# Instance norm over 512 volumes: loads and stores on two queues, six buffers, and a two-pass variance in one chain per tile

## The chip, the cores and the metric

The kernel runs on one core of one Trainium2 chip. The metric is device time in microseconds (us) of one execution; lower is better.

## The reference

The input `x` has shape (8, 64, 32, 64, 64) in float32: 512 instances (8 batches of 64 channels) of 131,072 elements each, 268.44 MB in all. Every instance is normalised by its own mean and variance.

```python
def reference(x, eps):                       # eps = 1e-5
    mean = np.mean(x, axis=(2, 3, 4), keepdims=True)
    var = np.var(x, axis=(2, 3, 4), keepdims=True)
    return ((x - mean) / np.sqrt(var + eps)).astype(np.float32)
```

## The kernel before

A tile is 128 partitions by 8192 elements (`F`), 4 MB in float32. It holds 8 instances, each spread over 16 partitions (`SPLIT`), and lies in one contiguous piece in memory, as 128 rows of 32 KB. The 64 tiles are worked through in one loop; `KPG` is 1, so a group is one tile.

For each tile, `issue_load` puts a load on SyncE's queue (SP). `issue_compute` then does the following:

- VectorE (DVE) sums all 8192 elements of a partition (L92), while ScalarE (ACT) squares them, writes the squares to a scratch tile that nobody reads, and collects their sum (L100).
- TensorE multiplies the two columns of sums with `ones_t`, a block matrix that adds up the 16 partitions of an instance and hands the result to each of them (L108).
- VectorE turns the totals into mean and mean of squares (L117), squares the mean (L128), and forms the variance plus eps as the difference (L131); ScalarE takes the root (L141); VectorE makes the reciprocal `scale` (L147) and `bias`, minus mean times scale (L149).
- The tile is scaled in place by three engines side by side: VectorE the first 1024 columns (L169), ScalarE the next 1024 (L161), GpSimd (POOL) the remaining 6144 (L169).

`issue_store` (L180) puts the store on the same SP queue. The main loop issues the store of tile g - 2 (`LAG`) after the load of tile g, so this one queue carries loads and stores in turn, and a store that waits for its tile's scaling holds back the load behind it. The pool `data` has four buffers, so the load of tile g also waits until the store of tile g - 4 has landed. The tile framework orders the instructions within each engine and adds the semaphores.

Of the kernel before, what the change touches and what calls it, by code (L numbers as in the profile page):

```python
# [1 line left out]

# [4 lines left out]


@with_exitstack
def kernel(  # L10
    ctx: ExitStack,
    tc: tile.TileContext,
    x: bass.AP,
    eps: bass.AP,
    out: bass.AP,
):
    nc = tc.nc
    fp32 = mybir.dt.float32

    P = 128  # L20
    B, C, D, H, W = x.shape
    n_inst = B * C
    n_elem = D * H * W

    eps_f = float(eps)

    SPLIT = 16
    IPT = P // SPLIT
    F = n_elem // SPLIT

    G = 8
    KPG = G // IPT
    n_groups = n_inst // G

    LAG = 2

    x_packed = x.rearrange("b c d h w -> (b c) (d h w)").rearrange(
        "(k i) (s f) -> k (i s) f", i=IPT, s=SPLIT
    )
    out_packed = out.rearrange("b c d h w -> (b c) (d h w)").rearrange(  # L40
        "(k i) (s f) -> k (i s) f", i=IPT, s=SPLIT
    )

    singles = ctx.enter_context(tc.tile_pool(name="singles", bufs=1))
    data_pool = ctx.enter_context(tc.tile_pool(name="data", bufs=4))
    scratch_pool = ctx.enter_context(tc.tile_pool(name="scratch", bufs=2))
    stat_pool = ctx.enter_context(tc.tile_pool(name="stats", bufs=4))
    psum_pool = ctx.enter_context(tc.tile_pool(name="psum", bufs=4, space=bass.MemoryType.PSUM))

    ones_t = singles.tile([P, P], fp32)  # L50
    nc.vector.memset(ones_t, 1.0 / SPLIT)  # L51
    blk_pattern = [[-SPLIT, P // SPLIT], [0, SPLIT]]
    nc.gpsimd.affine_select(  # L53
        out=ones_t,
        in_=ones_t,
        pattern=blk_pattern,
        compare_op=mybir.AluOpType.is_ge,
        fill=0.0,
        base=0,
        channel_multiplier=1,  # L60
    )
    nc.gpsimd.affine_select(  # L62
        out=ones_t,
        in_=ones_t,
        pattern=[[SPLIT, P // SPLIT], [0, SPLIT]],
        compare_op=mybir.AluOpType.is_ge,
        fill=0.0,
        base=SPLIT - 1,
        channel_multiplier=-1,
    )  # L70

    inv_F = 1.0 / F

    c1 = F // 8
    c2 = F // 4
    norm_splits = [
        (nc.vector, 0, c1),
        (nc.scalar, c1, c2),
        (nc.gpsimd, c2, F),
    ]  # L80

    def issue_load(g):
        x_tiles = data_pool.tile([P, KPG, F], fp32, name="x_tiles")
        src = x_packed[g * KPG : (g + 1) * KPG].rearrange("k p f -> p k f")
        nc.sync.dma_start(out=x_tiles, in_=src)
        return x_tiles

    def issue_compute(g, x_tiles):
        psums = stat_pool.tile([P, KPG, 2], fp32, name="psums")

        for k in range(KPG):
            nc.vector.reduce_sum(  # L92
                out=psums[:, k, 0:1],
                in_=x_tiles[:, k, :],
                axis=mybir.AxisListType.X,
            )
            sq_scratch = scratch_pool.tile(
                [P, F], mybir.dt.bfloat16, name="sq_scratch"
            )
            nc.scalar.activation(  # L100
                out=sq_scratch,
                in_=x_tiles[:, k, :],
                func=mybir.ActivationFunctionType.Square,
                accum_out=psums[:, k, 1:2],
            )

        tot = psum_pool.tile([P, KPG, 2], fp32, name="tot")
        nc.tensor.matmul(  # L108
            out=tot,
            lhsT=ones_t,  # L110
            rhs=psums,
            start=True,
            stop=True,
        )

        me2 = stat_pool.tile([P, KPG, 2], fp32, name="me2")
        nc.vector.tensor_scalar(  # L117
            out=me2,
            in0=tot,
            scalar1=inv_F,  # L120
            scalar2=None,
            op0=mybir.AluOpType.mult,
        )
        mean = me2[:, :, 0]
        e2 = me2[:, :, 1]

        msq = stat_pool.tile([P, KPG], fp32, name="msq")
        nc.vector.tensor_mul(out=msq, in0=mean, in1=mean)  # L128

        var_eps = stat_pool.tile([P, KPG], fp32, name="var_eps")  # L130
        nc.vector.scalar_tensor_tensor(  # L131
            out=var_eps,
            in0=e2,
            scalar=eps_f,
            in1=msq,
            op0=mybir.AluOpType.add,
            op1=mybir.AluOpType.subtract,
        )

        std = stat_pool.tile([P, KPG], fp32, name="std")  # L140
        nc.scalar.activation(  # L141
            out=std,
            in_=var_eps,
            func=mybir.ActivationFunctionType.Sqrt,
        )
        scale = stat_pool.tile([P, KPG], fp32, name="scale")
        nc.vector.reciprocal(out=scale, in_=std)  # L147
        bias = stat_pool.tile([P, KPG], fp32, name="bias")
        nc.vector.scalar_tensor_tensor(  # L149
            out=bias,  # L150
            in0=mean,
            scalar=-1.0,
            in1=scale,
            op0=mybir.AluOpType.mult,
            op1=mybir.AluOpType.mult,
        )

        for k in range(KPG):
            for eng, lo, hi in norm_splits:
                if eng is nc.scalar:  # L160
                    nc.scalar.activation(  # L161
                        out=x_tiles[:, k, lo:hi],
                        in_=x_tiles[:, k, lo:hi],
                        func=mybir.ActivationFunctionType.Identity,
                        scale=scale[:, k : k + 1],
                        bias=bias[:, k : k + 1],
                    )
                else:
                    eng.tensor_scalar(  # L169
                        out=x_tiles[:, k, lo:hi],  # L170
                        in0=x_tiles[:, k, lo:hi],
                        scalar1=scale[:, k : k + 1],
                        scalar2=bias[:, k : k + 1],
                        op0=mybir.AluOpType.mult,
                        op1=mybir.AluOpType.add,
                    )

    def issue_store(g, x_tiles):
        dst = out_packed[g * KPG : (g + 1) * KPG].rearrange("k p f -> p k f")
        nc.sync.dma_start(out=dst, in_=x_tiles)  # L180

    pending = {}
    for g in range(n_groups):
        x_tiles = issue_load(g)
        issue_compute(g, x_tiles)
        pending[g] = x_tiles
        if g >= LAG:
            issue_store(g - LAG, pending.pop(g - LAG))
    for g in range(n_groups - LAG, n_groups):
        issue_store(g, pending.pop(g))  # L190


# [1 line left out]
_INS = ['x', 'eps']  # L194
_OUTS = [((8, 64, 32, 64, 64), 'float32')]
#: Inputs that are plain numbers.
_NUMBERS = {'eps': 9.999999747378752e-06}


# [26 lines left out]
```

## Time and profile before

| | |
|---|---|
| median of 6 runs | 1251.45 us (1250.46 to 1254.96) |
| the profiled execution | 1253.22 us; its span 1251.4 us |
| VectorE busy | 659.2 us (53%) |
| ScalarE busy | 550.6 us (44%) |
| GpSimd busy | 380.3 us (30%) |
| TensorE busy | 35.7 us (3%) |
| moved by DMA | 536.99 MB, mean 429 GB/s over the span |

The span runs from the first to the last instruction of the profiled execution; the device time also holds a little that lies around it. In the profile's rows, a line number such as L92 is that of the kernel's source. A group's row gives the engine, the operation, output and input with partitions by elements and type, the count, the busy time with the mean of one in ns, and the time the engine stood idle ahead of these instructions with what ended it. A row of the table by stretches gives the stretch, its length, the busy time of PE (TensorE), PEld (its weight loads), DVE, ACT and POOL, then the clock that TensorE was granted, the share of the DMA engines, and GB/s. "SPq" is SyncE's DMA queue. In the page's slices each column is a fortieth of the span, 31.3 us.

### The profile page before, as it was taken

What the parts mean: (1) busy time and instruction counts of PE and PEld (TensorE: products, weight loads), DVE (VectorE), ACT (ScalarE), POOL (GpSimd) and SP (SyncE); (2) the same over time, 40 slices, a digit from 0 to 9 for tenths busy, and PEclk for the clock granted to TensorE, in tenths of its full rate; (3) what the DMA queues carried; (4) which work ended last, traced back from release to release, by engine and by line L of the source; (5) the groups of instructions that cost most, each with busy time, mean ns of one, the idle gap of its engine ahead of it and who ended that gap; (6) DMA issues with size and microseconds to landing.
All of it is one profiled execution on the core that took longest, in us unless ns stands there. A gap on an engine that the chain in (4) does not pass through costs nothing.

```text
span 1251.4 us, 1827 instructions
## 1 busy us (share of the span) xinstructions
PE 35.7 (3%) x128; PEld 32.0 (3%) x128; DVE 659.2 (53%) x449; ACT 550.6 (44%) x258; POOL 380.3 (30%) x70
## 2 busy tenths in 40 slices
PE   0000000000000000000000000000000000000000
PEld 0000000000000000000000000000000000000000
DVE  5736455464554645536456465464554645646543
ACT  5535445354453544535435344354453544535432
POOL 2332332313323233232331322313323233232231
DMA  9999999999999999999999999999999999999997
GB/s 402 418 434 434 432 430 430 430 434 434 435 430 430 435 430 435 436 435 426 434 435 432 435 434 435 430 433 434 432 435 434 434 427 436 433 434 435 435 431 332
DMA packets 18444, 536.99 MB, mean 429 GB/s; under 512 B 2048, under 2 KB 2048, under 8 KB 2048
## 3 DMA queue, kind: packets, MB, share of 16 engines
q1 hardware_dynamic: 18432, 536.88, 99.6%
q14 instruction: 11, 0.09, 0.0%
q8 instruction: 1, 0.02, 0.0%
HBM read 268.44 MB, written 268.44 MB: 429 GB/s over the span
## 4 chain that ended last, share of the span: by engine, by line
DMA 74%; issue 16%; POOL 7%; DVE 1%; POOLq 1%; PE 0%; ACT 0%
DMA out_dram<-x_tiles 39%; DMA x_tiles<-in_x_dram 35%; POOL x_tiles L169 7%; DVE psums L92 1%; POOLq L221 0%; DVE x_tiles L169 0%; POOLq L169 0%; PE tot L108 0%; ACT std L141 0%; DVE scale L147 0%; DVE var_eps L131 0%; DVE bias L149 0%; DVE msq L128 0%; DVE me L117 0%
## 5 line engine op out<-in xcount | busy, mean ns | idle before, releaser
L92 DVE TENSOR_REDUCE psums<-x_tiles 128x1 f32<-128x8192 f32 x64 | 555.9, 8686 | 494.5 <-DMA x_tiles<-in_x_dram 494.5
L100 ACT ACTIVATE sq_scratch<-x_tiles 128x8192 bf16<-128x8192 f32 x64 | 449.9, 7029 | 462.9 <-DMA x_tiles<-in_x_dram 462.9
L169 POOL TENSOR_SCALAR x_tiles<-x_tiles,scale,bias 128x6144 f32<-128x6144 f32 x64 | 379.4, 5929 | 857.0 <-DVE bias L149 635.3
L161 ACT ACTIVATE x_tiles<-x_tiles,bias,scale 128x1024 f32<-128x1024 f32 x64 | 79.4, 1241 | 40.5 <-DVE bias L149 40.5
L141 ACT ACTIVATE std<-var_eps 128x1 f32<-128x1 f32 x64 | 13.0, 203 | 178.8 <-DVE var_eps L131 178.8
L108 PE MATMUL tot<-psums,ones_t 128*128 128x2 f32 x128 | 35.7, 348 | 1195.2 <-DVE psums L92 1195.2
L108 PEld LDWEIGHTS tot<-psums,ones_t 128*128 128x128 f32 x128 | 32.0, 310 | 1198.8 <-issue 1198.8
L169 DVE TENSOR_SCALAR x_tiles<-x_tiles,scale,bias 128x1024 f32<-128x1024 f32 x64 | 52.0, 813 | 2.5 <-DVE bias L149 0.2
L117 DVE TENSOR_SCALAR me<-tot 128x2 f32<-128x2 f32 x64 | 10.2, 160 | 47.5 <-PE tot L108 47.5
L147 DVE RECIPROCAL scale<-std 128x1 f32<-128x1 f32 x64 | 10.5, 164 | 21.8 <-ACT std L141 21.8
L100 ACT ACTIVATION_READ_ACCUMULATOR sq_scratch<-x_tiles 128x1 f32 x64 | 11.9, 187 | 0.0
L131 DVE SCALAR_TENSOR_TENSOR var_eps<-me,msq 128x1 f32<-128x1 f32 x64 | 10.2, 160 | 2.2
L128 DVE TENSOR_TENSOR msq<-me 128x1 f32<-128x1 f32 x64 | 10.2, 159 | 2.2
L149 DVE SCALAR_TENSOR_TENSOR bias<-me,scale 128x1 f32<-128x1 f32 x64 | 10.2, 159 | 2.2
L100 ACT ACT_TABLE_LOAD x1 | 1.3, 1283 | 0.8 <-PEq L207 0.8
L141 ACT ACT_TABLE_LOAD x1 | 1.3, 1283 | 0.0
L51 DVE MEMSET ones_t<- 128x128 f32 x1 | 0.2, 165 | 0.9 <-PEq L207 0.9
L53 POOL TENSOR_SCALAR_AFFINE_SELECT ones_t<-ones_t 128x128 f32<-128x128 f32 x1 | 0.3, 343 | 0.6 <-DVE ones_t L51 0.6
L62 POOL TENSOR_SCALAR_AFFINE_SELECT ones_t<-ones_t 128x128 f32<-128x128 f32 x1 | 0.3, 338 | 0.1
L207 POOL MEMSET const-float32-0.0<- 128x1 f32 x1 | 0.1, 98 | 0.3 <-issue 0.3
L207 POOL MEMSET const-bfloat16-1.0<- 128x1 bf16 x1 | 0.1, 101 | 0.0
L207 POOL MEMSET const-uint8-127<- 128x1 uint8 x1 | 0.1, 101 | 0.0
(1 smaller groups left out, 0.1 us busy)
## 6 DMA issues: line engine op xcount, KB each, us to landing
x_tiles<-in_x_dram SPq DMA_DIRECT2D x64, 4096.0 KB, 29.0
out_dram<-x_tiles SPq DMA_DIRECT2D x64, 4096.0 KB, 31.5
```

The source lines that it names most:

```text
L92: nc.vector.reduce_sum(out=psums[:, k, 0:1], in_=x_tiles[:, k, :], axis=mybir.AxisListType.X,)
L100: nc.scalar.activation(out=sq_scratch, in_=x_tiles[:, k, :], func=mybir.ActivationFunctionType.Square, accum_out=psums[:, k, 1:2],)
L108: nc.tensor.matmul(out=tot, lhsT=ones_t, rhs=psums, start=True, stop=True,)
L117: nc.vector.tensor_scalar(out=me2, in0=tot, scalar1=inv_F, scalar2=None, op0=mybir.AluOpType.mult,)
L128: nc.vector.tensor_mul(out=msq, in0=mean, in1=mean)
L131: nc.vector.scalar_tensor_tensor(out=var_eps, in0=e2, scalar=eps_f, in1=msq, op0=mybir.AluOpType.add, op1=mybir.AluOpType.subtract,)
L141: nc.scalar.activation(out=std, in_=var_eps, func=mybir.ActivationFunctionType.Sqrt,)
L147: nc.vector.reciprocal(out=scale, in_=std)
L149: nc.vector.scalar_tensor_tensor(out=bias, in0=mean, scalar=-1.0, in1=scale, op0=mybir.AluOpType.mult, op1=mybir.AluOpType.mult,)
L161: nc.scalar.activation(out=x_tiles[:, k, lo:hi], in_=x_tiles[:, k, lo:hi], func=mybir.ActivationFunctionType.Identity, scale=scale[:, k : ...
L169: eng.tensor_scalar(out=x_tiles[:, k, lo:hi], in0=x_tiles[:, k, lo:hi], scalar1=scale[:, k : k + 1], scalar2=bias[:, k : k + 1], op0=mybir ...
L207: nc = _bacc.Bacc("TRN2", target_bir_lowering=False, num_devices=1)
```

## The change

The kernel is rewritten around the same tile of 128 by 8192. The parts that change:

- **Queues.** Loads stay on SP's queue (L77). The store of a tile is issued by ScalarE (L131), right after ScalarE's last instruction for that tile, with no lag.
- **Buffers.** The pool `data` has six buffers in place of four, so a load waits for the store six tiles back. The first six loads wait for nothing. A store also waits, on a shared semaphore, for the store four tiles back.
- **Statistics.** The mean comes first: VectorE sums the first half of the columns (L83), ScalarE the second half through `Identity` with an accumulator (L86), TensorE adds up the partitions (L93), and VectorE adds the two halves and negates (L95). Then ScalarE squares x minus mean over all 8192 columns with `neg_mean` as its bias (L103), TensorE adds up again (L107), ScalarE takes the root with eps as its bias, straight from PSUM (L109), and VectorE makes `scale` (L111) and `bias` (L113). What the two ScalarE passes write goes to one uint8 tile, `unused`, that nobody reads.
- **Scaling.** VectorE scales the second half of the columns (L114), ScalarE the first half (L122). GpSimd takes no part.
- **Order.** The loop stands under `tc.manual_schedule()`, so each engine runs its instructions as written: load, statistics, scaling and store of one tile, then the next tile.

On ScalarE one tile is L86, L103, L109, L122, L131; on VectorE L83, L95, L111, L113, L114; on TensorE L93, L107.

```diff
-    G = 8
-    KPG = G // IPT
-    n_groups = n_inst // G
-
-    LAG = 2
+    n_tiles = n_inst // IPT
+    SLOTS = 6
...
-    data_pool = ctx.enter_context(tc.tile_pool(name="data", bufs=4))
-    scratch_pool = ctx.enter_context(tc.tile_pool(name="scratch", bufs=2))
+    data_pool = ctx.enter_context(tc.tile_pool(name="data", bufs=SLOTS))
...
+    eps_t = singles.tile([P, 1], fp32, name="eps_t")
+    nc.vector.memset(eps_t, eps_f)
+    unused = singles.tile([P, F], mybir.dt.uint8, name="unused")
...
+    def load(g):
+        t = data_pool.tile([P, F], fp32, name="xt")
+        nc.sync.dma_start(out=t, in_=x_t[g])
+        return t
+
+    def compute(t):
+        cut = F // 2
+        sums = stat_pool.tile([P, 2], fp32, name="sums")
+        nc.vector.reduce_sum(
+            out=sums[:, 0:1], in_=t[:, :cut], axis=mybir.AxisListType.X
+        )
+        nc.scalar.activation(
+            out=unused[:, cut:],
+            in_=t[:, cut:],
+            func=Act.Identity,
+            accum_out=sums[:, 1:2],
+        )
+        mean_ps = psum_pool.tile([P, 2], fp32, name="mean_ps")
+        nc.tensor.matmul(out=mean_ps, lhsT=avg, rhs=sums, start=True, stop=True)
+        neg_mean = stat_pool.tile([P, 1], fp32, name="neg_mean")
+        nc.vector.tensor_reduce(
+            out=neg_mean,
+            in_=mean_ps,
+            axis=mybir.AxisListType.X,
+            op=Alu.add,
+            negate=True,
+        )
+        squares = stat_pool.tile([P, 1], fp32, name="squares")
+        nc.scalar.activation(
+            out=unused, in_=t, func=Act.Square, bias=neg_mean, accum_out=squares
+        )
+        var_ps = psum_pool.tile([P, 1], fp32, name="var_ps")
+        nc.tensor.matmul(out=var_ps, lhsT=avg, rhs=squares, start=True, stop=True)
+        std = stat_pool.tile([P, 1], fp32, name="std")
+        nc.scalar.activation(out=std, in_=var_ps, func=Act.Sqrt, bias=eps_t)
+        scale = stat_pool.tile([P, 1], fp32, name="scale")
+        nc.vector.reciprocal(out=scale, in_=std)
+        bias = stat_pool.tile([P, 1], fp32, name="bias")
+        nc.vector.tensor_mul(out=bias, in0=neg_mean, in1=scale)
+        nc.vector.tensor_scalar(
+            out=t[:, cut:],
+            in0=t[:, cut:],
+            scalar1=scale,
+            scalar2=bias,
+            op0=Alu.mult,
+            op1=Alu.add,
+        )
+        nc.scalar.activation(
+            out=t[:, :cut], in_=t[:, :cut], func=Act.Identity, scale=scale, bias=bias
+        )
+
+    with tc.manual_schedule():
+        for g in range(n_tiles):
+            t = load(g)
+            compute(t)
+            nc.scalar.dma_start(out=out_t[g], in_=t)
```

More of the change, by code (lines that the diff above doesn't have):

```diff
@@ L4 @@
 import concourse.tile as tile
-from concourse import bass_utils, mybir
+from concourse import mybir
 from concourse._compat import with_exitstack
@@ L18 @@
     fp32 = mybir.dt.float32
+    Alu = mybir.AluOpType
+    Act = mybir.ActivationFunctionType
     P = 128
@@ L29 @@
     F = n_elem // SPLIT
-    G = 8
-    KPG = G // IPT
-    n_groups = n_inst // G
-    LAG = 2
-    x_packed = x.rearrange("b c d h w -> (b c) (d h w)").rearrange(
+    n_tiles = n_inst // IPT
+    SLOTS = 6
+    x_t = x.rearrange("b c d h w -> (b c) (d h w)").rearrange(
         "(k i) (s f) -> k (i s) f", i=IPT, s=SPLIT
     )
-    out_packed = out.rearrange("b c d h w -> (b c) (d h w)").rearrange(
+    out_t = out.rearrange("b c d h w -> (b c) (d h w)").rearrange(
         "(k i) (s f) -> k (i s) f", i=IPT, s=SPLIT
@@ L44 @@
     singles = ctx.enter_context(tc.tile_pool(name="singles", bufs=1))
-    data_pool = ctx.enter_context(tc.tile_pool(name="data", bufs=4))
-    scratch_pool = ctx.enter_context(tc.tile_pool(name="scratch", bufs=2))
+    data_pool = ctx.enter_context(tc.tile_pool(name="data", bufs=SLOTS))
     stat_pool = ctx.enter_context(tc.tile_pool(name="stats", bufs=4))
[L48 to L52, printed above, removed]
+    psum_pool = ctx.enter_context(
+        tc.tile_pool(name="psum", bufs=2, space=bass.MemoryType.PSUM)
+    )
+    avg = singles.tile([P, P], fp32, name="avg")
+    nc.vector.memset(avg, 1.0 / n_elem)
     nc.gpsimd.affine_select(
[L54 to L57, printed above, removed]
+        out=avg,
+        in_=avg,
+        pattern=[[-SPLIT, IPT], [0, SPLIT]],
+        compare_op=Alu.is_ge,
         fill=0.0,
@@ L62 @@
     nc.gpsimd.affine_select(
[L63 to L66, printed above, removed]
+        out=avg,
+        in_=avg,
+        pattern=[[SPLIT, IPT], [0, SPLIT]],
+        compare_op=Alu.is_ge,
         fill=0.0,
@@ L70 @@
     )
[L72 to L113, printed above, removed]
-        )
[L116 to L122, printed above, removed]
-        )
[L124 to L137, printed above, removed]
-        )
[L140 to L190, printed above, removed]
+    eps_t = singles.tile([P, 1], fp32, name="eps_t")
```

## The prediction

> **What bounds the kernel now.** I read the page's slices first, then its queue part. The rows are the mean busy share of the sixteen DMA engines and what they moved, in forty slices; then the one queue that carries all tiles.
>
> ```profile
> DMA  9999999999999999999999999999999999999997
> GB/s 402 418 434 434 432 430 430 430 434 434 435 430 430 435 430 435 436 435 426 434 435 432 435 434 435 430 433 434 432 435 434 434 427 436 433 434 435 435 431 332
> q1 hardware_dynamic: 18432, 536.88, 99.6%
> ```
>
> The transfers fill the span. 536.88 MB must move in both kernels, so only three things can help: fewer idle microseconds at the two ends, or a better rate between. For the ends I read the busy table by stretches (last columns: clock, DMA share, GB/s).
>
> ```profile
> 0.00:4.00 4.00, 0.00 (x0) 0.00 (x0) 0.17 (x1) 1.28 (x1) 0.89 (x6) 1.00 0.67 205
> 4.00:30.00 26.00, 0.56 (x2) 0.50 (x2) 15.67 (x8) 14.73 (x6) 6.00 (x1) 1.00 1.00 432
> 30.00:70.00 40.00, 1.67 (x6) 1.50 (x6) 25.36 (x21) 20.60 (x12) 17.77 (x3) 1.00 1.00 420
> 715.25:1025.46 310.21, 8.90 (x32) 8.00 (x32) 164.81 (x112) 137.06 (x64) 94.92 (x16) 1.00 1.00 433
> 1232.00:1240.00 8.00, 0.00 (x0) 0.00 (x0) 0.97 (x2) 1.24 (x1) 5.93 (x1) 1.00 0.45 193
> ```
>
> Against 433 GB/s, the first 4 us lose 4 x (1 - 205/433) = 2.1 us (first bytes arriving), 30 to 70 loses 40 x (1 - 420/433) = 1.2, and 1232 to 1240 loses 8 x (1 - 193/433) = 4.4, where the last store is not yet issued. The pace per tile comes from the chain in order of time: these two pieces are one turn of four tiles apart, 77.42 us, so 19.36 us per tile.
>
> ```profile
> 715.25 31.50 DMA out_dram<-x_tiles
> 792.67 31.49 DMA out_dram<-x_tiles
> ```
>
> Compute must stay under that pace. The groups by line give the durations, the waits the hop through TensorE (47.5 / 64 = 0.74 us).
>
> ```profile
> L92 DVE TENSOR_REDUCE psums<-x_tiles 128x1 f32<-128x8192 f32 x64 | 555.9, 8686 | 494.5 <-DMA x_tiles<-in_x_dram 494.5
> L100 ACT ACTIVATE sq_scratch<-x_tiles 128x8192 bf16<-128x8192 f32 x64 | 449.9, 7029 | 462.9 <-DMA x_tiles<-in_x_dram 462.9
> L161 ACT ACTIVATE x_tiles<-x_tiles,bias,scale 128x1024 f32<-128x1024 f32 x64 | 79.4, 1241 | 40.5 <-DVE bias L149 40.5
> L141 ACT ACTIVATE std<-var_eps 128x1 f32<-128x1 f32 x64 | 13.0, 203 | 178.8 <-DVE var_eps L131 178.8
> L169 DVE TENSOR_SCALAR x_tiles<-x_tiles,scale,bias 128x1024 f32<-128x1024 f32 x64 | 52.0, 813 | 2.5 <-DVE bias L149 0.2
> L100 ACT ACTIVATION_READ_ACCUMULATOR sq_scratch<-x_tiles 128x1 f32 x64 | 11.9, 187 | 0.0
> DVE me L117 <- PE tot L108: 47.5, 64, 0.7
> ```
>
> **The change, part by part: the compute chain.** GpSimd loses its 6144-column share (5.9 us per tile). Sums, squares and scaling become one chain on VectorE and ScalarE with two trips through TensorE instead of one. ScalarE costs (7029 - 203)/8192 = 0.833 ns per element here. So the half-width sum is 0.20 + 3.41 + 0.19 (accumulator read) = 3.81 us. The squares take 7.03 + 0.09 + 0.19 = 7.31 (two pointer operands cost 1241 - 853 - 203 = 185 ns in the 1024-column row, so one costs 0.09). The half-width scaling is 1.24 + 3072 x 0.833 ns = 3.80. VectorE's half sum is 0.16 + (8.69 - 0.16)/2 = 4.42, its half scaling at most 4 x 0.81 = 3.25.
>
> ScalarE walks through all of it in fixed order, so its loop is the period: scaling 3.80, store issue 0.40 (0.34 on SP, plus hops), sum 3.81, TensorE 0.74, negated mean 0.21, squares 7.31, TensorE 0.74, square root 0.25, VectorE's reciprocal and product with hops 0.49: 17.8 us. VectorE starts the next sum while ScalarE still scales, so 3.25 + 4.42 = 7.7 lies beside 8.0 and costs nothing. Nothing shows these ScalarE shapes, nor a uint8 result or a store issued there. Bounds: each half at four times the 1024-column row is 4.96, the issue 0 to 0.8, so 17.4 to 20.7. I take 17.8, because the 8192-column row is nearest in kind. It leaves 1.6 us under 19.36, hidden by the transfers; if that cover goes, every microsecond over costs 64.
>
> **The queues.** Each store is now issued by ScalarE, after its own scaling, VectorE's half, and the store four tiles back. Behind it on ScalarE stands the next tile's sum, and VectorE and TensorE wait for that. A store four back lies 77 us back, so I cost the wait at nothing. SP keeps only loads: six go out with no wait, then each waits for the store six tiles back. No store stands ahead of a load in a ring any more.
>
> Start: load 0 lands at 13.15 as now. Its chain gives 13.2 + 4.42 + 0.95 + 7.31 + 1.30 (table load) + 0.25 + 0.49 + 3.80 + 0.40 = 32.1; first bytes move some 1.5 us later, as 2.1 us were lost at the start. By 33.5 the loads are (33.5 - 2.1)/9.68 = 3.2 tiles ahead, and queued, so the 1.2 us of 30 to 70 can go. Bounds 0 to 1.2; I take 1.2.
>
> Tail: if both rings share equally, that lead of 3.2 tiles stays to the end. When load 63 lands, 2.2 stores (21.7 us) stand before the last one; today it is two (19.4 us). From landing to issue it will be 18.4 us (the chain without overlap), where it was 16.9 (1221.50 to 1238.38). So the cover grows by 2.3 and the need by 1.5: 0.8 us of the 4.4 goes; all of it, if loads get a little more than their half and the backlog is deeper. I take the middle, 2.2 of 0.8 to 4.4; engines that run ahead of the slowest gain nothing, which argues against the upper end.
>
> Middle: from 90.33 to 637.83 the chain needs 547.5 us for 28 tiles, 5.6 more than at 19.36. I leave that as it is (0 to 5.6 gained). Rate with two rings: nothing in this trace runs two. From 715 on, engines already alternate loads and stores in one ring at 433. I take no change; ends are the best slice, 436, and the worst of the middle, 426: -8.5 to +20.4 us for 536.88 MB.
>
> A rule speaks against expecting more. The Trainium skill, "DMA: Bandwidth & Descriptors", Rules for kernel authors, says that spreading DMAs over several issuing engines does not help bandwidth, as all run on the same 16 engines; by it the split is worth nothing, and our 99.6% agrees. The same page, Latency and other measured facts, gives 214 GB/s per direction as full rate for copies through both hardware queues; by that, an estimate for this volume is 268.44 / 0.214 = 1254 us, about today's time. No run here shows it.
>
> **Sum.** -1.2 - 2.2 = -3.4. The profiled execution took 1253.2 (span 1251.4 and 1.8 around it), so 1249.8; that execution lies 1.8 above the median of the six runs, so 1248.0 against 1251.45.
>
> **Rivals.** (1) Slower: two rings cost the engines rate, because each switches between a read and a write stream at every 32 KB row. For it: where stores first meet loads, the table shows 420. Against: the even 433 later, with both kinds in flight. It decides once the rate falls by more than 0.3% (3.4 of 1240 us), under 431.8. At the lowest middle slice, 426, it costs 536.88/0.426 - 536.88/0.433 = 20.4: 1268. (2) No difference: the engine that is latest at load 63 has no idle time to give back, the start gains nothing: 1249 to 1254. For it: the 4.4 is a mean over sixteen engines. (3) The chain becomes the bound: it decides from 19.36; at 20.7 it costs 1.3 x 64 = 83, some 1330; at 19.6, 15, some 1265. Against it: it takes the 1024-column row for 4096 columns. (4) Stores win more than their half: no backlog is left and the last chain lies bare. Then only one store covers 18.4 us, some 8 to 10 more idle: 1256 to 1261.
>
> **Chances.** Forecast, 1242 to 1248.9: 0.42. Rival 1: 0.25; rival 2: 0.20; rival 3: 0.07; rival 4: 0.06. A run of this kernel can tell 0.2%, 2.5 us, from no change. Rivals 1, 3 and 4 are slower: 0.38. The range reaches from the forecast's low end (all of the 4.4 and 1.2 and most of the 5.6 gained) to rival 1 at 426: 1242 to 1268; its ends leave out part of 1 and most of 3. The forecast's own range is 1242 to 1249.
>
> **What would show it.** Right: two queues with about 268 MB each, together over 99%; the 30 to 70 stretch at 430 or more; stores issued about 19.4 us apart; ScalarE waiting for loads at its half-width sum; the stretch before the last store less empty. Wrong: DMA slices in the middle under 430 (rival 1); ScalarE without load waits, idle DMA in mid-span (rival 3); a last store issued with both rings dry for 8 us or more (rival 4). Equal slices and a time inside 1249 to 1254 make it rival 2.

## The result and the profile after

The changed kernel takes 1249.48 us (median of 22 runs, 1248.40 to 1251.69), the kernel before 1251.85 (44 runs): a ratio of 0.998, 95% interval 0.9974 to 0.9985, so 1.9 to 3.3 us less. Forecast were 3.4 less. 1249.48 lies 0.6 us above the forecast's own range (1242 to 1248.9) and inside the band that the prediction gave to rival 2, no difference (1249 to 1254); what tells it from rival 2 is that the interval leaves out no change. The profiled spans are 1248.8 and 1251.4.

From the page of the changed kernel, the slices, the two queues, and the last part, whose last column is the median time from issue to landing:

```profile
DMA  9999999999999999999999999999999999999998
GB/s 403 420 437 434 431 429 436 435 435 431 429 435 436 435 431 430 433 436 435 429 431 436 436 435 429 431 435 436 435 429 431 434 436 433 430 432 433 437 435 348
...
q1 hardware_dynamic: 9216, 268.44, 49.9%
q10 hardware_dynamic: 9216, 268.44, 49.8%
...
xt<-in_x_dram SPq DMA_DIRECT2D x64, 4096.0 KB, 50.9
out_dram<-xt ACTq DMA_DIRECT2D x64, 4096.0 KB, 47.4
```

The transfers still fill the span, now from two rings with half of the bytes each. A store needs 47.4 us to land; in the kernel before it was 31.5. While loads and stores share the engines, the pace is 19.36 us per tile, so 47.4 us means that a finished tile queues behind more than one other. That backlog is the lead of the loads, seen from the other side.

The same stretches as in the prediction, of the changed kernel, with two more that the account below needs, from 90 to 404 us and the last one. First these two of the kernel before:

```profile
90.33:404.49 314.16, 8.92 (x32) 8.01 (x32) 164.81 (x112) 137.07 (x64) 94.59 (x16) 1.00 1.00 432
...
1240.00:1251.40 11.40, 0.00 (x0) 0.00 (x0) 0.00 (x0) 0.00 (x0) 0.00 (x0) 1.00 0.76 328
```

Then those of the changed kernel:

```profile
0.00:4.00 4.00, 0.00 (x0) 0.00 (x0) 0.17 (x2) 1.28 (x1) 0.89 (x6) 1.00 0.72 229
4.00:30.00 26.00, 1.14 (x4) 1.00 (x4) 6.96 (x5) 14.47 (x7) 0.00 (x0) 1.00 0.99 429
30.00:70.00 40.00, 2.35 (x8) 2.01 (x8) 19.13 (x12) 34.52 (x14) 0.00 (x0) 1.00 1.00 422
...
90.33:404.49 314.16, 19.64 (x68) 17.04 (x68) 123.57 (x84) 253.83 (x102) 0.00 (x0) 1.00 1.00 434
...
715.25:1025.46 310.21, 17.74 (x62) 15.52 (x62) 117.06 (x80) 239.79 (x96) 0.00 (x0) 1.00 1.00 433
...
1232.00:1240.00 8.00, 0.00 (x0) 0.00 (x0) 0.00 (x0) 1.10 (x1) 0.00 (x0) 1.00 0.90 385
1240.00:1248.80 8.80, 0.00 (x0) 0.00 (x0) 0.00 (x0) 0.00 (x0) 0.00 (x0) 1.00 0.45 194
```

Bytes give the balance. Still to move at 1232 us were 4.79 MB in the changed kernel (8 x 385 + 8.8 x 194 in kB) and 5.28 MB in the kernel before (8 x 193 + 11.4 x 328), 1.1 us of work less. From 1232 to the end the changed kernel needs 16.8 us, of which 4.79 MB at 433 GB/s are 11.1, so 5.7 idle; the kernel before 19.4, of which 12.2 are work, so 7.2 idle. That is 1.1 from all that lies ahead of 1232 and 1.5 from the tail: the 2.6 by which the spans differ. It is a balance of means over sixteen engines; the rates are whole numbers, and half a GB/s over the 1232 us is 1.4 us, so the split is taken from the bytes still to move, not from the middle's rates.

The groups of the changed kernel:

```profile
L103 ACT ACTIVATE unused<-xt,neg_mean 128x8192 uint8<-128x8192 f32 x64 | 455.8, 7121 | 100.6 <-DVE neg_mean L95 100.6
L83 DVE TENSOR_REDUCE sums<-xt 128x1 f32<-128x4096 f32 x64 | 282.8, 4419 | 167.5 <-DMA xt<-in_x_dram 167.5
L86 ACT ACTIVATE unused<-xt 128x4096 uint8<-128x4096 f32 x64 | 231.5, 3617 | 96.0 <-DMA xt<-in_x_dram 91.4
L122 ACT ACTIVATE xt<-xt,bias,scale 128x4096 f32<-128x4096 f32 x64 | 243.3, 3801 | 31.3 <-DVE bias L113 31.3
...
L114 DVE TENSOR_SCALAR xt<-xt,scale,bias 128x4096 f32<-128x4096 f32 x64 | 154.4, 2413 | 2.7 <-DVE bias L113 0.3
```

Both engines wait for loads ahead of their half sums (167.5 and 91.4 us): the chain is faster than the transfers. While the first tiles lie ready it runs at its own pace, as two lines of its timeline show, 17.5 us apart:

```profile
36.90 7.12 ACT L103 ACTIVATE unused<-xt,neg_mean 128x8192 uint8<-128x8192 f32 x1 [0.93 <-DVE neg_mean L95]
...
54.40 7.12 ACT L103 ACTIVATE unused<-xt,neg_mean 128x8192 uint8<-128x8192 f32 x1 [0.93 <-DVE neg_mean L95]
```

The end of the changed kernel in steps of 1 us shows what bounds it now:

```profile
1242.00:1243.00 1.00, 0.00 (x0) 0.00 (x0) 0.00 (x0) 0.00 (x0) 0.00 (x0) 1.00 1.22 524
1243.00:1244.00 1.00, 0.00 (x0) 0.00 (x0) 0.00 (x0) 0.00 (x0) 0.00 (x0) 1.00 0.16 66
1244.00:1245.00 1.00, 0.00 (x0) 0.00 (x0) 0.00 (x0) 0.00 (x0) 0.00 (x0) 1.00 0.08 33
...
1246.00:1247.00 1.00, 0.00 (x0) 0.00 (x0) 0.00 (x0) 0.00 (x0) 0.00 (x0) 1.00 0.08 33
```

A sixteenth of 433 GB/s is 27. So from about 1243.5 on about one of the sixteen DMA engines works, for some 3.5 us, and the others are done.

The trace also records when each of the sixteen engines has landed its share of a transfer. In us, the median engine and the last one (load 63 and store 63 are those of the last tile, store 62 that of the tile before it):

| | load 63: median, last | store 62: median, last | store 63 issued | store 63: median, last |
|---|---|---|---|---|
| before | 1214.4, 1221.5 | 1233.8, 1240.9 | 1238.38 | 1249.4, 1250.5 |
| changed | 1211.6, 1215.2 | 1233.6, 1238.3 | 1233.13 | 1244.2, 1248.0 |
| four buffers (e2 below) | 1219.2, 1220.2 | 1234.2, 1237.2 | 1238.06 | 1249.1, 1249.2 |

In the kernel before, the last engine is 7 us behind the median. It still works on store 62 when store 63 is issued, so it has no idle time in the gap that the other engines show, and its share of store 63 lands 9.6 us after that of store 62, which is one share at full rate (9.68). In the changed kernel the last engine is 3.7 us behind; it too has no idle time there (9.7 us), and it sets the end.

### The profile page after: what moved, and what is told of

The parts are those of the page before. It is cut to its first block, busy times and chain, and to the rows that moved or that the text cites. A ratio compares the mean times of both kernels' runs of the same rounds, so it can differ in the third digit from the quotient of the medians.

```text
span 1248.8 us, 1828 instructions
## 1 busy us (share of the span) xinstructions
PE 73.5 (6%) x256; PEld 64.1 (5%) x256; DVE 467.4 (37%) x322; ACT 961.7 (77%) x386; POOL 0.9 (0%) x6
## 4 chain that ended last, share of the span: by engine, by line
ACT 45%; DVE 31%; another core or an unknown queue 12%; PE 6%; issue 2%; DMA 1%; ACTq 0%
ACT unused L103 37%; DVE sums L83 19%; DVE xt L114 10%; ACT xt L122 4%; ACT unused L86 3%; PE var_ps L107 3%; PE mean_ps L93 3%; ACT std L109 1%; DMA xt<-in_x_dram 1%; DVE scale L111 1%; DVE neg_mean L95 1%; DVE bias L113 1%; ACTq L131 0%; ACT L109 0%
## 5 line engine op out<-in xcount | busy, mean ns | idle before, releaser
L103 ACT ACTIVATE unused<-xt,neg_mean 128x8192 uint8<-128x8192 f32 x64 | 455.8, 7121 | 100.6 <-DVE neg_mean L95 100.6
L83 DVE TENSOR_REDUCE sums<-xt 128x1 f32<-128x4096 f32 x64 | 282.8, 4419 | 167.5 <-DMA xt<-in_x_dram 167.5
L86 ACT ACTIVATE unused<-xt 128x4096 uint8<-128x4096 f32 x64 | 231.5, 3617 | 96.0 <-DMA xt<-in_x_dram 91.4
L122 ACT ACTIVATE xt<-xt,bias,scale 128x4096 f32<-128x4096 f32 x64 | 243.3, 3801 | 31.3 <-DVE bias L113 31.3
L111 DVE RECIPROCAL scale<-std 128x1 f32<-128x1 f32 x64 | 10.5, 164 | 530.9 <-ACT std L109 530.9
L114 DVE TENSOR_SCALAR xt<-xt,scale,bias 128x4096 f32<-128x4096 f32 x64 | 154.4, 2413 | 2.7 <-DVE bias L113 0.3
L93 PE MATMUL mean_ps<-sums,avg 128*128 128x2 f32 x128 | 36.0, 351 | 670.9 <-DVE sums L83 573.9
L93 PEld LDWEIGHTS mean_ps<-sums,avg 128*128 128x128 f32 x128 | 32.0, 311 | 674.7 <-ACT unused L86 656.9
L107 PE MATMUL var_ps<-squares,avg 128*128 128x1 f32 x128 | 37.6, 362 | 484.1 <-ACT unused L103 484.1
L107 PEld LDWEIGHTS var_ps<-squares,avg 128*128 128x128 f32 x128 | 32.1, 311 | 489.6 <-ACT unused L103 489.6
L109 ACT ACTIVATE std<-var_ps,eps_t 128x1 f32<-128x1 f32 x64 | 16.8, 262 | 42.7 <-PE var_ps L107 42.7
L95 DVE TENSOR_REDUCE neg_mean<-mean_ps 128x1 f32<-128x2 f32 x64 | 10.2, 160 | 60.2 <-PE mean_ps L93 60.2
L103 ACT ACTIVATION_READ_ACCUMULATOR unused<-xt,neg_mean 128x1 f32 x64 | 11.9, 187 | 0.0
L86 ACT ACTIVATION_READ_ACCUMULATOR unused<-xt 128x1 f32 x64 | 11.9, 186 | 0.0
L113 DVE TENSOR_TENSOR bias<-neg_mean,scale 128x1 f32<-128x1 f32 x64 | 10.2, 160 | 2.2
## 6 DMA issues: line engine op xcount, KB each, us to landing
out_dram<-xt ACTq DMA_DIRECT2D x64, 4096.0 KB, 47.4
```

What stands on the lines that cost most here:

```text
L83: nc.vector.reduce_sum(out=sums[:, 0:1], in_=t[:, :cut], axis=mybir.AxisListType.X)
L86: nc.scalar.activation(out=unused[:, cut:], in_=t[:, cut:], func=Act.Identity, accum_out=sums[:, 1:2],)
L93: nc.tensor.matmul(out=mean_ps, lhsT=avg, rhs=sums, start=True, stop=True)
L95: nc.vector.tensor_reduce(out=neg_mean, in_=mean_ps, axis=mybir.AxisListType.X, op=Alu.add, negate=True,)
L103: nc.scalar.activation(out=unused, in_=t, func=Act.Square, bias=neg_mean, accum_out=squares)
L107: nc.tensor.matmul(out=var_ps, lhsT=avg, rhs=squares, start=True, stop=True)
```

## The experiments

The theories: **A**, the tail gains, because in a ring of their own the loads run ahead; **B**, the middle gains, because two rings end an early slow stretch; **C**, what is left at the end is one late engine that also carries the instruction fetches (the transfers on the queue that the profile names instruction, 8 KB each); **D**, the new arithmetic gains.

**One ring (e1).** Stores go back to SP's queue, two tiles late:

```diff
-            nc.scalar.dma_start(out=out_t[g], in_=t)
+            pending[g] = t
+            if g >= 2:
+                nc.sync.dma_start(out=out_t[g - 2], in_=pending.pop(g - 2))
...
```

> The changed kernel with its stores back on SP's queue, each issued two tiles late, so that loads and stores share one ring again; six buffers, chain and order stay. Theory A (the gain lies in the tail: in a ring of their own the loads run ahead, so more stores stand before the last one): the cover before the last store is two stores again while the chain from landing to issue is 17.9 us, so the gap returns and the time is 1250.5 to 1253; the stretch before the last store falls under 300 GB/s. Theory B (the middle: two rings end the slow stretch of the first 400 us, 432 against 434 GB/s): 1251 to 1252, with 432 from 90 to 404 us and no emptier tail. Theory D (compute is what gained: GpSimd's share gone, chain shorter): stays at 1249.5.

Measured: 1254.01, ratio to the kernel before 1.0017 (1.0008 to 1.0025). It lies 4.5 above the changed kernel; the new arithmetic and six buffers give nothing in one ring, so D doesn't hold by itself. Two of its stretches:

```profile
90.33:404.49 314.16, 18.96 (x66) 16.55 (x66) 119.33 (x83) 245.78 (x100) 0.00 (x0) 1.00 1.00 431
...
1232.00:1240.00 8.00, 0.58 (x2) 0.50 (x2) 2.74 (x3) 6.85 (x4) 0.00 (x0) 1.00 0.54 233
```

Both gaps are back: 431 early, as B says, and 233 near the end, as A says. The two don't exclude each other here.

**Four buffers (e2).** `SLOTS = 4`, nothing else.

> The changed kernel with four buffers in place of six. Theory A: with four, load g starts after store g-4 has landed; one turn of a buffer is load 21 + chain 18 + store 21 = 60 us of the 77 that four tiles take, so both rings stay fed, but the loads' lead falls from 3.2 to at most 2.9 tiles: 1249.3 to 1251. Theory B: no change, 1249.5. Theory D': the buffers are the gain: 1251.5 or more.

Measured: 1252.47, ratio 1.0005 (0.9996 to 1.0014): no gain over the kernel before is left, though both rings are there. Its lines, from the page's last part and the table by stretches:

```profile
out_dram<-xt ACTq DMA_DIRECT2D x64, 4096.0 KB, 35.3
```

```profile
90.33:404.49 314.16, 19.01 (x66) 16.54 (x66) 119.48 (x83) 250.01 (x100) 0.00 (x0) 1.00 1.00 433
...
1232.00:1240.00 8.00, 0.59 (x2) 0.50 (x2) 2.74 (x3) 4.87 (x4) 0.00 (x0) 1.00 0.38 164
```

The middle runs at 433 early and late; the tail is as empty as before the change (164 GB/s against 193). So A is needed: without the lead the gain is gone. B alone gives no gain, but what it is worth beside A is not separated. The landing times say that it is real: at 460 us the latest engine is 6.1 us behind the median in the kernel before and 4.3 in e1, with one ring, and 1.0 and 1.2 in the changed kernel and here, with two. In the kernel before, an engine that is 7 us late would have set the end at 1250.5 even with a full tail; no run has the lead and that lateness. My size was off: with four buffers the backlog falls by 12 us (47.4 to 35.3), not by 0.3 tiles.

**Stores on ScalarE alone, free order (e3).** One line of the kernel before:

```diff
-        nc.sync.dma_start(out=dst, in_=x_tiles)
+        nc.scalar.dma_start(out=dst, in_=x_tiles)
```

> The kernel before with one edit: its stores are issued by ScalarE in place of SP, so loads and stores have a ring each; GpSimd still scales, four buffers, one-pass variance. Theories A and B: most of the gain appears, 1248.5 to 1250.5, unless ScalarE's queue holds a store back behind a 7.0 us squaring, which four buffers with 14 us to spare should cover. Theory D (compute): no gain, 1251.9.

Measured: 1503.45, ratio 1.2008 (1.1991 to 1.2024). I had missed this by 250 us. The source issues the store of tile g - 2 behind the work on tile g (`LAG`), and on ScalarE that work stands ahead of the store. In its timeline two tiles' stores go out together, after a wait of 20.7 us for a load:

```profile
591.98 8.69 DVE L92 TENSOR_REDUCE psums<-x_tiles 128x1 f32<-128x8192 f32 x1 [20.71 <-DMA x_tiles<-in_x_dram]
...
601.88 5.24 DVE L128 TENSOR_TENSOR msq<-me 128x1 f32<-128x1 f32 x1
...
607.35 0.34 ACTq L180 DMA_DIRECT2D out_dram<-x_tiles  x1
...
608.28 0.34 ACTq L180 DMA_DIRECT2D out_dram<-x_tiles  x1
```

The next such wait ends at 639.25, 47.3 us later, so two tiles take 47.3 us where the transfers would take 38.7. Each load waits for a store, and each store for work on ScalarE that stands ahead of it and that waits for a load: tile 26 is scaled at 614.20 and its store goes out at 654.62, behind the squares of tiles 27 and 28. Every other store is held for some 40 us in this way. A part of the loss may be the product L128, which takes 5.24 us here: the square root that stands ahead of a store waits for it. The two were not separated.

**The same in fixed order (e5).** The edit of e3, and the loop of the changed kernel, which has no lag (the old loop goes out):

```diff
...
+    with tc.manual_schedule():
+        for g in range(n_groups):
+            x_tiles = issue_load(g)
+            issue_compute(g, x_tiles)
+            issue_store(g, x_tiles)
```

> The kernel before with its stores on ScalarE, as in the run of 1503 us, but in fixed order: load, compute and store of one tile, then the next tile (no lag, four buffers, GpSimd still scales). Theory E (that run lost its time because the free order put the next tile's 7.0 us squaring, which waits for a load, ahead of a finished store on ScalarE, while that load waits for the store): the loss goes and the time is that of the changed kernel with four buffers, 1251.5 to 1254. Rival (stores on ScalarE collide with GpSimd's scaling, whatever the order): 1400 or more.

Measured: 1253.41, ratio 1.0015 (1.0007 to 1.0024). Order and lag make the difference of 250 us: a store now goes out 0.03 us after its tile is scaled, in the mean of 64. The lag went together with the free order, so which of the two cost it is not separated; in e3 no store stands behind the squares of more tiles than the lag of two puts there. With four buffers, the old arithmetic (1253.4) and the new one (1252.5) are within 1 us of each other.

**Transfers alone (e4).** `compute(t)` is taken out of the loop.

> The changed kernel without any arithmetic: each tile is loaded on SP's queue and stored as it is on ScalarE's; statistics and scaling are left out. Theory A (transfers set the time, compute shows only in the tail): 1243 to 1247, with 433 GB/s in the middle. Theory C (one late DMA engine, behind the others by about 3 us at the end because it also carries the instruction fetches): with hardly any instructions to fetch, all engines end within 1 us of each other, and the time is at the lower end, 1243 to 1245. If the late engine has another cause, the thin end of some 3 us stays.

Measured: 1247.68, ratio 0.9964 (0.9951 to 0.9976). All arithmetic together costs the changed kernel 1.8 us. (The rows have no columns for PE, PEld and ACT, which do nothing here.) The table by steps at its end:

```profile
1242.00:1243.00 1.00, 0.00 (x0) 0.00 (x0) 1.00 0.31 131
1243.00:1244.00 1.00, 0.00 (x0) 0.00 (x0) 1.00 0.08 33
1244.00:1245.00 1.00, 0.00 (x0) 0.00 (x0) 1.00 0.00 0
```

The thin end lasts about 1 us in place of 3.5, and the page shows 2 transfers on the queue named instruction, where the changed kernel has 9 on it and 2 more on another. The landing times show what these two do. One is fetched at 712.9 us: between the loads before and after it an engine falls from 0.2 to 0.9 us behind the median. The other comes at 733.1: the latest engine falls from 1.2 to 1.9. So a fetch makes an engine some 0.7 us late, which fits C; the 1.1 that the latest engine had before the first fetch have another cause, which stays open.

**A dose of fetches (e6).** 64 copies of one column per tile on GpSimd:

```diff
...
+            for _ in range(64):
+                nc.gpsimd.tensor_copy(out=dose, in_=scale)
```

> The changed kernel with 64 copies of one column per tile added on GpSimd, 4096 instructions that nobody waits for and that use no data queue. Theory C (the instruction fetches ride on one DMA engine, which ends late; at 27.1 GB/s, a sixteenth of 433, a fetch of 8 KB costs it 0.30 us): 4096 instructions of 64 bytes are 32 fetches more, 9.7 us on that engine, so 1258 to 1262, with a thin end of some 13 us; twice that if every copy brings a semaphore instruction with it. Rival 1 (the late engine has another cause, or the fetches spread over all sixteen): 1249.5 to 1250.5. Rival 2 (GpSimd work disturbs the others): the middle falls under 433 evenly on all engines.

Measured: 1265.82, ratio 1.0107 (1.0093 to 1.0122). From its page, and from its table by steps (between 1242 and 1248 three such steps follow each other):

```profile
q14 instruction: 42, 0.34, 0.1%
```

```profile
1244.00:1246.00 2.00, 0.00 (x0) 0.00 (x0) 1.93 (x3) 1.58 (x1) 1.66 (x2) 1.00 0.08 33
```

There are 33 fetches more (32 were expected), and for 6 us about one engine works and the others stand still; the middle stays at 433. At the last load two engines are far behind the median, by 18.4 and 9.9 us, where the changed kernel has 3.7 and 2.8: 21.8 us more, or 0.66 for each of the 33, near the 0.7 of e4, where nothing was copied. So C holds with a correction: the fetches fell on two engines, not on one, and the later one sets the end. Rival 1 and 2 fall. The size is larger: 16.3 us for 33 is 0.49 each, not 0.30. The last tile counts as landed only when the late engine has its share; its chain starts at 1230.32 and its store goes out at 1248.26, 15.1 us later than in the changed kernel, while the others have run dry.

**Slack of the chain (e7, e8).** One more pass of 1300 or 3400 columns on ScalarE behind the store:

```diff
+            nc.scalar.activation(out=unused[:, :1300], in_=unused[:, :1300], func=Act.Identity)
```

> The changed kernel with one more ScalarE pass per tile over 1300 columns of the tile that nobody reads, behind the store: 0.20 + 1300 x 0.833 ns = 1.28 us, so ScalarE's loop of 17.5 us becomes 18.8, under the 19.36 that the transfers take. My account (the loop is hidden up to 19.36): no change beyond the tail, 1249.5 to 1251. Rival (the loop already sets part of the pace): about 64 x 1.28 = 82 us more.

Measured: 1249.37, ratio 0.9983 (0.9974 to 0.9993): 82 us more of ScalarE work, 1.29 a tile on a loop of 17.5, cost nothing.

> The same with 3400 columns: 3.03 us more per tile, a loop of 20.5, which is 1.2 over 19.36. My account: ScalarE becomes the bound, 13.3 us for the first load, 64 x 20.5, and some 12 for the last store: about 1338 (1330 to 1345), ScalarE without waits for loads, and DMA below nine tenths. Rival (a slower chain only eats into the backlog): under 1260.

Measured: 1332.66, ratio 1.0642 (1.0628 to 1.0655). ScalarE waits for only one load, the first. The point at which the chain takes over lies between 18.8 and 20.5 us, around the 19.36 of the rows. A stretch of e8, ScalarE busy for 272 of 311 us:

```profile
404.49:715.25 310.76, 18.19 (x62) 15.53 (x62) 108.50 (x76) 271.93 (x108) 0.00 (x0) 1.00 0.99 412
```

DMA share stays at 0.99 though the rate falls to 412; a full share doesn't prove a full rate. There I was wrong: I had expected it under nine tenths.

**The old arithmetic with six buffers (e9).** The edits of e5, and two more:

```diff
-    data_pool = ctx.enter_context(tc.tile_pool(name="data", bufs=4))
-    scratch_pool = ctx.enter_context(tc.tile_pool(name="scratch", bufs=2))
+    data_pool = ctx.enter_context(tc.tile_pool(name="data", bufs=6))
+    scratch_pool = ctx.enter_context(tc.tile_pool(name="scratch", bufs=1))
...
-                [P, F], mybir.dt.bfloat16, name="sq_scratch"
+                [P, F], mybir.dt.uint8, name="sq_scratch"
```

> The kernel before with four edits and none of the new arithmetic: stores on ScalarE, fixed order, six buffers, and one uint8 tile for the unread squares (to make room). Its one-pass variance, its chain with GpSimd and its splits stay. Theory A (queues, order and lead are the gain; the two-pass chain is worth nothing in time): 1249 to 1250.5, as the changed kernel. Theory D (the new chain matters): 1251.5 or more, near the 1253.4 that it took with four buffers.

Measured: 1284.54, ratio 1.027 (1.0256 to 1.0284). Neither theory foresaw this. The page's two queues (SP's loads on q1, the stores on q10):

```profile
q1 hardware_dynamic: 9216, 268.44, 50.7%
q10 hardware_dynamic: 9216, 268.44, 48.6%
```

Its middle runs at 421 to 425 GB/s at a full share, and it is the loads whose transfers take longer. Backlog and chain are in order: a store lands after 45.8 us, and both engines wait for loads. At the last load the sixteen engines are spread over 21 us, against 4.7 in the changed kernel. What slows the loads stays open: GpSimd's scaling, the place of the buffers and the uint8 tile behind them were not separated. In the trace, load packets of more than 1.3 us (the usual one takes 1.21) are rarer beside GpSimd's scaling, 10% against 17%, which speaks against a direct collision with it. As it is, the old arithmetic doesn't reach the changed kernel's time with these queues and buffers, and this run can't say whether the arithmetic is why.

**Five buffers (e10).** `SLOTS = 5`.

> The changed kernel with five buffers. Theory A (with four buffers the loads' lead was cut and the gap before the last store opened; six bring 1249.5, four 1252.5): in between or already at the floor, 1249.3 to 1251, with the stretch from 1232 to 1240 between the 164 GB/s of four buffers and the 385 of six.

Measured: 1249.11, ratio 0.9982 (0.9973 to 0.9991), a store's time to landing 47.5 us and 414 GB/s from 1232 to 1240. Five buffers carry the whole lead, the sixth does nothing.

**No chain on the last tile (e11).**

```diff
-            compute(t)
+            if g < n_tiles - 1:
+                compute(t)
```

> The changed kernel without the arithmetic of the last tile: tile 63 is loaded and stored as it is, its statistics and scaling are left out, so its store is issued as soon as it has landed. Theory C (the end is set by the one late DMA engine, which has a backlog of its own at that point): 1248.5 to 1249.5, a gain under 1 us. Rival (the end is set by the last chain of 18 us): all of what is left of the gap, 1.5 to 2 us, down to the 1247.7 of the run without arithmetic.

Measured: 1249.38, ratio 0.9986 (0.9977 to 0.9995). The last chain of 17.9 us costs nothing any more. C again: the late engine has its own work until then.

**A leaner version (e12).** Queues, buffers and order of the changed kernel; one pass, and fewer instructions (shortened):

```diff
+        nc.vector.reduce_sum(out=sums[:, 0:1], in_=t, axis=mybir.AxisListType.X)
+        nc.scalar.activation(
+            out=unused, in_=t, func=Act.Square, accum_out=sums[:, 1:2]
+        )
...
+        nc.vector.tensor_scalar(
+            out=t, in0=t, scalar1=scale, scalar2=bias, op0=Alu.mult, op1=Alu.add
+        )
```

> A version built from the findings: queues, six buffers and fixed order of the changed kernel, but one pass and as few instructions as I can make it. VectorE sums the whole row, ScalarE squares it once, one trip through TensorE, variance as mean of squares minus squared mean, VectorE scales the whole tile; about 15 instructions per tile in place of 21, GpSimd idle. Its VectorE loop is 8.69 + 0.74 + 1.0 + 0.3 + 4.6 + 0.4 = 15.7, under 19.36. Theory C (what is left over the floor is fetches on the late engine): two or three fetches fewer, each 0.3 to 0.5 us: 1248 to 1249.2. Rival (no fetch effect at this size): 1249.5; if its shorter first chain gives the loads less lead, up to 1250.5.

Measured: 1249.20, ratio 0.9982 (0.9973 to 0.9991); 1317 instructions in the trace in place of 1828, but only two fetches fewer. It is not to be told from the changed kernel. One pass or two, with these queues and buffers the time is the same, so the two-pass variance gains nothing. What it leaves open of D is GpSimd: it scales in neither kernel, and e9, where it does, is 35 us slower for a cause that is not known.

## Why the prediction was right, point by point

- **What bounds it, and the rate with two rings.** Right: 433 GB/s from 715 to 1025 in both. Rival 1 did not come, but e9 (421 to 425) shows that a loss of that size exists.
- **The chain.** Estimated 17.8, measured 17.5. L86 3.62, L103 7.12, L122 3.80 and L83 4.42 came out as worked out; L114 took 2.41, under the bound of 3.25. That it is hidden at 18.8 and no more at 20.5 is shown by e7 and e8, so rival 3 had its point about right.
- **Start, -1.2 us: failed.** From 30 to 70 us the rate went from 420 to 422, which is 0.2 us. Six queued loads did not lift it, so loads missing from the queue were not its cause. What the cause is stays open; in e4 that stretch runs at 433, but 4 to 30 falls to 407.
- **Tail, -2.2 of 0.8 to 4.4: right in kind, 1.5 in the mean of the engines.** This table has the start of the last tile's sums, the issue of the last store and the end of the span, in us:

| | last tile starts | last store issued | span | issue to end |
|---|---|---|---|---|
| before | 1221.50 | 1238.38 | 1251.4 | 13.0 |
| changed | 1215.26 | 1233.13 | 1248.8 | 15.7 |
| four buffers (e2) | 1220.18 | 1238.06 | 1250.0 | 11.9 |
| old arithmetic, four buffers (e5) | 1222.61 | 1239.50 | 1251.4 | 11.9 |

In the changed kernel the last load is 6.2 us earlier, and the last store still has work ahead of it (15.7 us to the end, where a store into empty rings takes 11.9). The working had a hole: in the kernel before, a cover of 19.4 us against a need of 16.9 leaves no gap at all, yet 4.4 us were there. What it left out is the lateness of the last engine: a chain starts when the last share has landed, 7 us after the median engine, which has by then 7 us less of stores before it. In the changed kernel the cover is 22.0 us (median engine, 1211.6 to 1233.6), near the 21.7 of the text, and the need 17.9 plus 3.7 of lateness, so the median engine has no gap left. The caveat of the text, that engines ahead of the slowest gain nothing, was the right one: the last engine sets the end, it had no idle time to give back in the kernel before (rival 2's condition), and e11 shows that the last chain is no longer on the path. As it is busy through the tail in both kernels, the 2.5 us by which it ends earlier (1250.5 to 1248.0) were gained ahead of the tail, where it falls behind less; the prediction didn't have this.
- **Middle, 0 (0 to 5.6 gained).** Of the 1.1 us gained ahead of 1232, 0.2 are the start's, so 0.9 came from there.
- **The sum.** 3.4 were forecast, 2.6 came in the spans and 2.4 in the medians. That it is this near owes something to luck: the start gave almost nothing, the middle, set at nothing, gave nearly as much, and the tail came out though its working left out the engines' lateness. By the prediction's own sign the time alone would make it rival 2.
- **Rival 4.** It didn't come. Its end, a last chain that lies bare, came in e2 for another reason, too few buffers, and cost 3.0 us, not 8 to 10.
- **The store on ScalarE, at nothing.** Right, with fixed order and no lag. I named what stands behind the store; what could stand ahead of it I had not weighed, and e3 shows that it can cost 250 us.

The rule of the Trainium skill ("DMA: Bandwidth & Descriptors", Rules for kernel authors), that issuing from several engines brings no bandwidth, agrees with 433 GB/s in both kernels. The gain of the two rings is not bandwidth but lead (which transfer may pass which) and, as far as the landing times tell, engines that stay closer together. That page's 214 GB/s per direction (Latency and other measured facts), which it measured on copies with rows of 16 KiB, is a little under what the rows here show with 32 KB, 216.5 (half of 433); the measurement decides.

## What to carry to other kernels

When transfers fill the span, look at the two ends and at how far loads may run ahead of stores: a ring for each, and just enough buffers for the lead (five here, four lose it). Put stores on a compute engine's queue only in an order where nothing that waits for a load stands ahead of a finished store. Count the instructions of engines off the path too: each fetch made a DMA engine some 0.7 us late (e4, e6), and the latest engine sets the end. And don't take a gap in the mean over sixteen engines for idle time of the one that ends last.

## What was not expected of the hardware

- Instruction fetches ride on a few of the DMA engines that move the data: 33 more of 8 KB made two engines later by 14.7 and 7.1 us and the program longer by 16.3, with about 33 GB/s, one engine's worth, moving near the end.
- The DMA engines drift apart: at the last load the latest is 7.0 us (before) and 4.4 (e1) behind the median with one ring, 3.7 (changed) and 1.0 (e2) with two.
- In e3 a VectorE product of one column with itself (L128) took 5.24 us, and 2536 ns in the mean of 64, beside GpSimd's scaling; in fixed order (e5), where GpSimd is idle by then, it takes 159 ns. The Trainium skill, "SBUF — State Buffer", Who interferes with whom, says that a VectorE instruction with two SBUF inputs contends with a GpSimd instruction that reads SBUF, and the row agrees.
- The DMA share stays at 0.99 to 1.00 while the rate falls to 412 (e8) or 421 (e9): transfers stretch, and only the GB/s column shows it.
